# A feed-forward layer's first products taken by blocks: seven 2x2x2 block products (Strassen's scheme) in place of eight

## The chip, the cores and the metric

One core of a Trainium2 chip runs the whole program. The metric is the device time of one execution in microseconds. TensorE (PE) multiplies, VectorE (DVE), ScalarE (ACT) and GpSimd (POOL) do the element-wise work, SyncE (SP) issues the DMAs. Weights and activations lie in SBUF, matmul results in eight PSUM banks of 128 x 512 fp32.

## The reference

Two layers over 512 latent tokens and 256 context tokens, width 1024. Each layer has a mixing part and a gated feed-forward part; the last layer computes the latent tokens alone. What the change touches is the feed-forward part of the last layer:

```python
def swiglu(h, w1, w3, w2):
    return (jax.nn.silu(h @ w1) * (h @ w3)) @ w2

x = x + g_f * swiglu(ada_modulate(x, norm_ffn, sh_f, sc_f), ffn_w1, ffn_w3, ffn_w2)
```

`h` is 512 x 1024, `w1` and `w3` are 1024 x 2816 (22 blocks of 128 features), `w2` is 2816 x 1024. `ada_modulate` is an RMS norm with a scale and a shift per channel.

## The kernel before

Activations lie feature-major: a tile holds 128 channels by all tokens, and there are eight such tiles (k = 0 to 7). Every fp32 product is made of three TensorE matmuls in the fp32r format: each operand is split into a high part (an ACT copy, rounded) and a low part (source less high part, a DVE or POOL subtraction), and `mm3` (line 181) adds high x high, low x high and high x low into one PSUM bank:

```python
def mm3(o, lh, ll, rh, rl, start, stop):
    mm(o, lh, rh, start, False)
    mm(o, ll, rh, False, False)
    mm(o, lh, rl, False, stop)
```

The helpers `mm` (L179 in the profile), `tt` (L187), `stt` (L190) and `act` (L193) stand for nearly all instructions, so the profile is read by tiles more than by lines. `split` (line 195) is the ACT copy and the subtraction.

The feed-forward part (from line 1281) runs in three parts of the 22 features, `FF_PARTS` (line 32): first the w1 and w3 products of the part's features, with a gate after each (`gate_up`, line 1326: tanh on ACT, two DVE multiplications, a split into a `g` tile), then the part's w2 products, whose sums are added to the residual tiles `xl` on DVE. A w1 or w3 product of one feature block is 8 k-steps of `mm3` over 512 tokens: 24 matmuls of 512 columns into one bank (`up_k`, line 1321). Weights come by `fload` and `w13` (lines 1293 and 1296): a DMA on SP's queue into a `raw` tile of 128 x 1024 (a ring of 3), then a split into a `whl` tile (a ring of 6 in the last layer). The w2 weights come in the same way.

The start of the last layer's feed-forward part is by halves of 256 tokens, since its input is made by halves: the mixing part's output projection ends with the products of the second half (from line 1262), while the norm of the first half is already summed up (`norm_add`, `norm_sums`, `norm_spread`, lines 361 to 395) and its tiles are modulated (`norm_mod`, line 405). Two feature blocks are multiplied with the first half, then the norm of the second half is spread by a matmul, then the same two with the second half. The first weights (`W_first`, line 1304) are loaded early, at the priority of the projection, and their low parts are made on POOL.

A planner (the tile framework, with a simulated time line) sets the order of instructions on each engine from the order of the program, priorities and its own estimates; the feed-forward part has no order of TensorE written out by hand. Each engine's queue, and SP's, then runs in that order. Rings (`bufs` of a pool) give a tile out again when all that used it is done.

## Time and profile before

| what | value |
|---|---|
| runs (3) | median 1691.22 us, 1690.29 to 1695.56 |
| the profiled execution | 1694.43 us |
| its span | 1692.6 us, 25083 instructions |
| granted TensorE clock, mean | 0.988 |
| TensorE matmuls | 1638.8 us busy, 97% of the span, 9924 recorded |
| DVE, ACT, POOL | 920.2, 578.6 and 238.7 us busy |
| last layer's feed-forward part | 1325.66 us to the end of the span, 366.94 us |

Busy time is the union of an engine's instructions, without its waits for semaphores. In a time line, consecutive instructions of one group are merged into a row: start, length, engine, line, operation, out<-in with shapes, count, and in brackets the idle time before it with what ended it. A table by stage gives, for each stretch, its length and then the busy time and count of each engine, the granted clock, the DMA share and the rate. A group row gives busy time and mean nanoseconds of one.

### The profile page before, as it was taken

Reading aid. Unit: us, or ns where it says so; the run is one execution under the profiler, and the core shown is the slowest. Engines: PE = TensorE matmul, PEld = TensorE weight load, DVE = VectorE, ACT = ScalarE, POOL = GpSimd, SP = SyncE. Lnnn points to the kernel's source line nnn. Section 1 sums busy time; section 2 is a strip of 40 time slices with the busy share of each in tenths; the row PEclk is TensorE's granted clock in tenths of the full one; section 3 lists DMA queues with packets and bytes.
Section 4 is the critical chain, followed back from the end, with each engine's and each line's share of the span. In section 5 each row is a group of like instructions: output and inputs, shape, how many; then the busy total and the mean of one; then the engine's idle time right before and its main releaser. Section 6 shows DMA issues by size and latency. Waiting matters only on the chain.

```text
span 1692.6 us, 25083 instructions
## 1 busy us (share of the span) xinstructions
PE 1638.8 (97%) x9924; PEld 1418.1 (84%) x9924; DVE 920.2 (54%) x1651; ACT 578.6 (34%) x1023; POOL 238.7 (14%) x280
## 2 busy tenths in 40 slices
PE   6999999799899999999999999999989899999999
PEld 5888988688788888888888889899777888888887
DVE  5799765677755563553433443453567553343332
ACT  4474224445434311221122324831445432222220
POOL 0143431003212300000000011332102200000000
PEclk9999999899899999999999999999999999999999
DMA  9545535834033362442411301322773143223321
GB/s 326 172 153 162 179 97 163 231 85 129 30 125 125 125 187 88 135 146 79 138 63 55 117 35 39 94 80 71 201 181 116 56 137 100 90 90 106 101 85 52
DMA packets 81394, 200.66 MB, mean 119 GB/s; under 512 B 10680, under 2 KB 26876, under 8 KB 80252
## 3 DMA queue, kind: packets, MB, share of 16 engines
q1 hardware_dynamic: 81276, 199.06, 38.0%
q8 instruction: 78, 1.28, 0.3%
q14 instruction: 40, 0.33, 0.1%
HBM read 172.81 MB, written 12.85 MB: 110 GB/s over the span
## 4 chain that ended last, share of the span: by engine, by line
PE 87%; DMA 4%; DVE 4%; ACT 2%; issue 1%; SPq 1%; POOL 0%; DVEq 0%; ACTq 0%; POOLq 0%
PE a L179 29%; PE m L179 25%; PE b L179 21%; PE y L179 11%; PE b L1184 1%; DMA st<-kt 1%; DVE u L190 1%; DVE whl L187 1%; DMA st<-qt 1%; DMA vn<-scr_v 0%; DVE adac L190 0%; DVE nacc L187 0%; DMA qn<-scr_q 0%; DMA adaw<-in_ada 0%; DMA raw<-in_wg 0%
## 5 line engine op out<-in xcount | busy, mean ns | idle before, releaser
L193 ACT ACTIVATE whl<-raw 128x1024 fp32r<-128x1024 f32 (+7 forms) x222 | 204.8, 927 | 386.9 <-PE a L179 142.6
L179 PE MATMUL m<-u,whl 128*128 128x512 f32 (+1 forms) x1278 | 266.5, 360 | 1.9 <-DVE whl L187 1.3
L187 DVE TENSOR_TENSOR whl<-raw,whl 128x1024 fp32r<-128x1024 f32 (+7 forms) x201 | 224.5, 1118 | 79.7 <-ACT whl L193 79.5
L179 PE MATMUL a<-u,whl 128*128 128x512 f32 (+1 forms) x1299 | 248.2, 347 | 3.1 <-ACT u L193 2.4
L179 PEld LDWEIGHTS m<-u,whl 128*128 128x128 f32 x1278 | 213.0, 192 | 36.4 <-DVE whl L187 1.9
L179 PEld LDWEIGHTS a<-u,whl 128*128 128x128 f32 x1299 | 210.0, 190 | 34.7 <-ACT u L193 2.8
L179 PE MATMUL b<-u,whl 128*128 128x512 f32 (+1 forms) x915 | 184.2, 352 | 3.1 <-DVE whl L187 1.8
L190 DVE SCALAR_TENSOR_TENSOR adac<-adaw,u,adac 128x512 f32<-128x512 f32 x196 | 158.0, 828 | 34.4 <-DMA adaw<-in_adaw 33.2
L179 PEld LDWEIGHTS b<-u,whl 128*128 128x128 f32 x915 | 151.6, 192 | 26.7 <-DVE whl L187 2.4
L179 PE MATMUL b<-whl,u 128*128 128x384 f32 (+1 forms) x696 | 144.4, 343 | 1.7 <-DVE u L190 0.9
L179 PE MATMUL m<-whl,u 128*128 128x384 f32 (+2 forms) x672 | 140.3, 344 | 0.5 <-ACT u L193 0.5
L179 PEld LDWEIGHTS b<-whl,u 128*128 128x128 f32 x696 | 122.0, 188 | 8.2 <-issue 3.9
L179 PE MATMUL a<-g,whl 128*128 128x512 f32 (+1 forms) x594 | 126.7, 370 | 0.0
L179 PEld LDWEIGHTS m<-whl,u 128*128 128x128 f32 x672 | 116.0, 188 | 12.1 <-issue 7.9
L179 PEld LDWEIGHTS a<-g,whl 128*128 128x128 f32 x594 | 103.9, 189 | 19.4 <-DVE ft L190 0.8
L190 DVE SCALAR_TENSOR_TENSOR ft<-ft,a 128x512 f32<-128x512 f32 (+1 forms) x53 | 30.5, 575 | 99.7 <-ACT ft L193 65.3
L179 PE MATMUL y<-u,whl 128*128 128x512 f32 (+1 forms) x420 | 82.5, 349 | 0.1
L179 PEld LDWEIGHTS y<-u,whl 128*128 128x128 f32 x420 | 68.1, 189 | 12.2 <-issue 1.7
L179 PE MATMUL m<-g,whl 128*128 128x512 f32 (+1 forms) x396 | 77.8, 350 | 0.0
L187 POOL TENSOR_TENSOR nacc<-nacc,nsq 128x256 f32<-128x256 f32 (+1 forms) x21 | 21.0, 1001 | 391.4 <-ACT nsq L193 391.2
L179 PEld LDWEIGHTS m<-g,whl 128*128 128x128 f32 x396 | 64.7, 189 | 9.7
L179 PE MATMUL b<-g,whl 128*128 128x256 f32 (+1 forms) x396 | 72.5, 336 | 0.0
(207 smaller groups left out, 2004.7 us busy)
## 6 DMA issues: line engine op xcount, KB each, us to landing
raw<-in_w SPq DMA_DIRECT2D x104, 512.0 KB, 3.7
adaw<-in_adaw SPq DMA_DIRECT2D x48, 512.0 KB, 4.7
adaw<-in_adaw SPq DMA_DIRECT2D x64, 256.0 KB, 2.8
raw<-in_wg SPq DMA_DIRECT2D x40, 384.0 KB, 3.6
raw<-in_w SPq DMA_DIRECT2D x32, 448.0 KB, 3.3
st<-kt SPq DMA_DIRECT2D x48, 192.0 KB, 6.2
adaw<-in_ada SPq DMA_DIRECT2D x8, 1024.0 KB, 10.0
raw<-in_woa SPq DMA_DIRECT2D x16, 320.0 KB, 5.4
```

The lines of the kernel that those rows point to most:

```text
L179: T.matmul(o, lhsT=l, rhs=r, start=start, stop=stop, skip_group_check=True)
L187: e.tensor_tensor(out=o, in0=a, in1=b, op=op)
L190: V.scalar_tensor_tensor(out=o, in0=a, scalar=s, in1=b, op0=op0, op1=op1)
L193: S.activation(out=o, in_=i, func=f, **kw)
L1184: T.transpose(ps[:, 128 * j:128 * j + 128], p[:, 128 * j:128 * j + 128], ident)
```

## The change

In the last layer, a new function `feed_forward_blocks` takes the place of the whole feed-forward part. It takes the features by pairs (11 pairs). For each pair, the matrix (2 feature blocks) x (2 halves of the 1024 channels) is multiplied with the matrix (2 halves of the channels) x (2 halves of the tokens) by Strassen's scheme in Winograd's form: seven products of blocks instead of eight, with sums of weight blocks (S) and of activation blocks (T) made before, and sums of products made after. A block product is, for w1 and w3 (w) and four k-steps (i), one `mm3` over 256 columns, 24 matmuls; both w lie in one bank.

- Weights: a pair loads four chunks of 128 x 1024 (`chunk`); POOL makes s3 = a11 - a21, s1 = a21 + a22, then S2 = s1 - a11 and S4 = a12 - S2 in place; each of the seven is split by ACT and DVE (`unit`). The `raw` ring has 6 places, the ring of split units (`wu`) 4.
- Activations: the T operands of the seven products are made once (`ops`), from `scaled`, `shifted` and `plain`, and kept.
- Sums of products: three banks X, Y, Z per pair. X takes products 1, 6, 7 and 4 in turn, Z products 5 and 3; between them ACT takes snapshots (`snap`), and DVE and POOL add a bank or a snapshot to another into the tiles `cm`, on which the gate works.
- The first two pairs run together, product by product in the order 1, 2, 5, 6, 3, 7, 4, so that the first two products need the first half of the tokens only; their first weights lie in spare `g` tiles and are split on POOL. The other pairs run one by one in the order 1, 5, 6, 2, 7, 3, 4.
- The parts are 8, 8 and 6 features instead of 8, 7 and 7, in both layers.

The diff, cut where a step is plain:

```diff
-FF_PARTS = ((0, 8), (8, 15), (15, 22))
+FF_PARTS = ((0, 8), (8, 16), (16, 22))
...
+        def feed_forward_blocks():
...
+            gtile = lambda: mk(gpool, [128, 2, TL], F32R, "g", 8)
+            def chunk(f, kh, spare=False):
+                raw = flat(gtile()).bitcast(F32) if spare else mk(wp, [128, 1024], F32, "raw", 6)
+                nc.sync.dma_start(out=raw, in_=d["w13"][l, f, :, :, 4 * kh:4 * kh + 4])
+                return raw
+            def unit(raw, e=V):
+                u = mk(wp, [128, 2, 1024], F32R, "wu", 4)
+                n = raw.shape[-1]
+                split(raw, u[:, 0, :n], u[:, 1, :n], e)
+                return u[:, :, :n].rearrange("p q (w k c) -> p q w k c", w=2, c=128)
+            class Pair:
+                def __init__(self, p, kinds, spare=False, e=V):
+                    self.p, self.kinds = p, kinds
+                    self.a11, self.a12 = chunk(2 * p, 0, spare), chunk(2 * p, 1, spare)
+                    self.u = {}
+                    if spare:
+                        self.u[1], self.u[2] = unit(self.a11, e), unit(self.a12, e)
+                    self.cm = [mk(tp, [128, 2, 2, 256], F32, "cm", 2) for _ in range(2)]
+                def rest(self):
+                    a21, a22 = chunk(2 * self.p + 1, 0), chunk(2 * self.p + 1, 1)
+                    if 1 not in self.u:
+                        self.u[1] = unit(self.a11)
+                    s3 = mk(wp, [128, 1024], F32, "raw", 6)
+                    tt(G, s3, self.a11, a21, ALU.subtract)
+                    tt(G, a21, a21, a22, ALU.add)
+                    self.s1, self.s3, self.a22 = a21, s3, a22
+                def weights(self, n):
+                    if n == 6:
+                        tt(G, self.a11, self.s1, self.a11, ALU.subtract)
+                    if n == 3:
+                        tt(G, self.a12, self.a12, self.a11, ALU.subtract)
+                    if n not in self.u:
+                        self.u[n] = unit({2: self.a12, 3: self.a12, 4: self.a22, 5: self.s1, 6: self.a11, 7: self.s3}[n])
+                    return self.u.pop(n)
...
+                def after(self, n):
+                    ab = lambda a: a.rearrange("p (w c) -> p w c", w=2)
+                    if n == 1:
+                        self.snap("p1", self.X)
+                    if n == 5:
+                        self.snap("p5", self.Z)
+                    if n == 6:
+                        self.snap("u1", self.X)
+                    if n == 2:
+                        tt(V, self.cm[0][:, :, 0], ab(self.Y), ab(self.p1), ALU.add)
+                    if n == 7:
+                        self.snap("u2", self.X)
+                        tt(G, self.cm[1][:, :, 1], ab(self.u2), ab(self.p5), ALU.add)
+                    if n == 3:
+                        tt(V, self.cm[0][:, :, 1], ab(self.Z), ab(self.u1), ALU.add)
+                        self.gate(0)
+                    if n == 4:
+                        act(self.cm[1][:, :, 0], ab(self.X), AF.Copy)
+                        self.gate(1)
...
+            def products(pairs, n, outer=False):
+                us = [p.weights(n) for p in pairs]
+                bs = [p.bank(n) for p in pairs]
+                for iis in [(i,) for i in range(4)] if outer else [range(4)]:
+                    for p, u, (bank, first) in zip(pairs, us, bs):
+                        for w in range(2):
+                            for i in iis:
+                                mm3(bank[:, 256 * w:256 * w + 256], u[:, 0, w, i], u[:, 1, w, i], ops[n][i][:, 0],
+                                    ops[n][i][:, 1], first and w == i == 0, i == 3)
+                for p in pairs:
+                    p.after(n)
...
+            products(two, 1, True)
+            sums = norm_sums((accs[1], 256), np0)
+            for p in two:
+                p.rest()
+            products(two, 2, True)
+            rb2 = norm_spread(sums, np0)
+            for i in four:
+                scaled(i, 1, 0, rb2)
+                tt(V, t[i][:, 0], t[i][:, 2], t[i][:, 0], ALU.subtract)
+                plain(5, i, 0)
+            products(two, 5, True)
+            for i in four:
+                scaled(i, 1, 1, rb2)
+                shifted(3, i, 3)
+                stt(t[i][:, 2], t[i][:, 3], between[:, i:i + 1], t[i][:, 2], ALU.add, ALU.subtract)
+                stt(t[i][:, 3], t[i][:, 3], sh(i + 4), t[i][:, 0], ALU.add, ALU.subtract)
+                plain(6, i, 3)
+            products(two, 6, True)
+            products(two, 3)
...
+            for pi, (f0, f1) in enumerate(FF_PARTS):
+                for p in range(f0 // 2, f1 // 2):
...
+                    q = Pair(p, {"X": bank, "Y": bank, "Z": bank})
+                    q.rest()
+                    for n in (1, 5, 6, 2, 7, 3, 4):
+                        products([q], n)
...
```

What is left out: the gate, which works as before but from the `cm` tiles; `shifted` (ACT adds the shift, DVE makes the low part) and `plain` (a split); the T operands of products 7 and 4; and the w2 stage, which loads its weights by halves of the part's features instead of by output blocks and is the same otherwise.

## Rows read from the trace of the kernel before

**Rows 1.** Page: TensorE's busy time, and the chain that ended last by engine.

```profile
PE 1638.8 (97%) x9924; PEld 1418.1 (84%) x9924; DVE 920.2 (54%) x1651; ACT 578.6 (34%) x1023; POOL 238.7 (14%) x280
...
PE 87%; DMA 4%; DVE 4%; ACT 2%; issue 1%; SPq 1%; POOL 0%; DVEq 0%; ACTq 0%; POOLq 0%
```

**Rows 2.** Table by stage: start, w1/w3 of part two, last w2, sum.

```profile
1325.66:1373.06 47.40, 46.28 (x297) 42.15 (x298) 28.14 (x57) 18.84 (x34) 1.86 (x3) 1.00 0.26 83
...
1460.10:1536.26 76.16, 76.16 (x338) 63.07 (x337) 29.79 (x34) 20.82 (x27) 0.00 (x0) 1.00 0.29 90
...
1650.49:1692.60 42.11, 38.25 (x169) 31.34 (x167) 10.54 (x13) 3.38 (x4) 0.00 (x0) 1.00 0.13 51
sum 366.94, PE 361.96 PEld 303.23 DVE 148.20 ACT 94.06 POOL 1.86; mean PE 51.71 PEld 43.32 DVE 21.17 ACT 13.44 POOL 0.27
```

**Rows 3.** Time line of TensorE: 68 matmuls of 256 columns, then groups of 512.

```profile
1345.60 8.32 PE L179 MATMUL a<-u,whl 128*128 128x256 f32 x68
1353.76 4.27 PE L179 MATMUL b<-u,whl 128*128 128x512 f32 x18
...
1460.10 5.60 PE L179 MATMUL b<-u,whl 128*128 128x512 f32 x24
1465.54 5.60 PE L179 MATMUL m<-u,whl 128*128 128x512 f32 x24
```

**Rows 4.** Time line of TensorE, start: first matmul, second norm's spread, first operand.

```profile
1325.66 0.50 PE L179 MATMUL b<-u,whl 128*128 128x256 f32 x2 [0.91 <-ACT u L193]
...
1337.91 0.61 PE L179 MATMUL a<-ndg,u 128*128 128x128 f32 x4
...
1339.62 0.74 PE L179 MATMUL a<-u,whl 128*128 128x256 f32 x4 [1.11 <-ACT u L193]
```

**Rows 5.** Time lines of POOL (two rows), then of DVE over the same time.

```profile
1304.49 2.40 POOL L187 TENSOR_TENSOR whl<-raw,whl 128x1024 fp32r<-128x1024 f32 x1 [8.50 <-ACT whl L193]
1307.23 4.96 POOL L187 TENSOR_TENSOR whl<-raw,whl 128x1024 fp32r<-128x1024 f32 x2 [0.34 <-ACT whl L193]
...
1307.49 0.47 DVE L190 SCALAR_TENSOR_TENSOR u<-b,u,u 128x256 f32<-128x256 f32 x1
1307.88 2.04 DVE L187 TENSOR_TENSOR nacc<-nacc,nsq 128x256 f32<-128x256 f32 x1
...
1310.25 2.22 DVE L187 TENSOR_TENSOR nacc<-nacc,nsq 128x256 f32<-128x256 f32 x1
...
1312.79 0.41 DVE L187 TENSOR_TENSOR nacc<-nacc,nsq 128x256 f32<-128x256 f32 x1
```

**Rows 6.** Groups by form: DVE, ACT; last, POOL's 128x512 (minimum/median/maximum ns).

```profile
L187 DVE TENSOR_TENSOR whl<-raw,whl 128x1024 fp32r<-128x1024 f32 x46 | 56.3, 1225 | 23.6 <-ACT whl L193 23.6
L187 DVE TENSOR_TENSOR g<-ft,g 128x512 fp32r<-128x512 f32 x20 | 13.7, 683 | 0.0
L190 DVE SCALAR_TENSOR_TENSOR ft<-ft,a 128x512 f32<-128x512 f32 x15 | 10.3, 688 | 44.6 <-ACT ft L193 31.1 <-PE a L179 13.4
L190 DVE SCALAR_TENSOR_TENSOR nt<-u,u,rb 128x512 f32<-128x512 f32 x8 | 6.0, 752 | 0.4
L190 DVE SCALAR_TENSOR_TENSOR u<-nt,u,u 128x256 fp32r<-128x256 f32 x16 | 7.3, 488 | 0.8 <-ACT u L193 0.8
L193 ACT ACTIVATE whl<-raw 128x1024 fp32r<-128x1024 f32 x104 | 109.6, 1056 | 248.7 <-PE a L179 97.3 <-PE m L179 63.3 <-PE b L179 32.7
L193 ACT ACTIVATE ft<-a 128x512 f32<-128x512 f32 x17 | 10.2, 597 | 58.2 <-PE a L179 58.2
L187 POOL TENSOR_TENSOR asum<-u,u x10: 1284/1290/1747, 175.1 to 1179.7; 128x512 f32<-128x512 f32 x10
```

**Rows 7.** DMA issues: KB each, median us from issue to landing.

```profile
raw<-in_w SPq DMA_DIRECT2D x104, 512.0 KB, 3.7
```

**Rows 8.** Time line of TensorE at the border of the layers.

```profile
1007.31 0.79 PE L179 MATMUL b<-whl,u 128*128 128x384 f32 x3 [0.89 <-DVE u L190]
```

More of the change, by code (lines that the diff above doesn't have):

```diff
@@ L1281, in hybrid_kernel @@
+        if last:
+            feed_forward_blocks()
+            xst.close()
+            continue
         p4_ = ExitStack()
```

71 lines of the change are left out of this document (added).

## Prediction

> **What bounds the kernel now.** I read the page first. TensorE is busy for 97% of the span and holds 87% of the chain that ended last [rows 1]. Then the table by stage, cut where the last layer's feed-forward begins and at its parts: the granted clock is 1.00 (the 2.4 GHz level) in each stage, and TensorE is busy for 46.28 of the first 47.40 us, all of a w1/w3 stage and all but the output tail of the last stage [rows 2]. So in this stretch of 366.94 us only fewer or shorter matmuls help, unless something new makes TensorE wait. The TensorE timeline gives the pace: a group of 24 matmuls of 512 columns starts 5.44 us after the one before, 226.7 ns each; the 68 matmuls of 256 columns that begin at 1345.60 end with the next group at 1353.76, 120.0 ns each [rows 3]. Last I read VectorE (DVE) and GpSimd (POOL) where both work, since the change gives both much to do.
>
> **What TensorE saves.** The change touches the last layer's 11 pairs of features. A pair took 2x2x8x3 = 96 matmuls of 512 columns, 21.76 us; seven block products of 2x4x3 = 24 matmuls of 256 columns are 168, 20.16 us (2.88 us a product). Ten pairs save 1.60 us each; the first, which already ran as 192 matmuls of 256 columns (23.04 us), saves 2.88. Together 18.9 us. The w2 products are as many as before (8x22x3), so their three stages and the tail stay at 123.7 us.
>
> By the Trainium skill (TensorE: Matmul & The Clock Gate, "Back-to-back issue gap") an isolated matmul's spacing is columns / 2.4 + 2.5 ns, 215.8 and 109.2 ns; by that the saving would be 26.3 us. The rows have about 13 ns above the columns' own time, which weighs on twice as many instructions; they decide, and the sum stays at 18.9.
>
> **What is added, and where it lies.** A steady pair (the nine after the first two) now gives POOL four additions of 128x1024 and one of 128x512; DVE seven weight splits (four before), two additions of a PSUM bank to a snapshot, four multiplications and two splits for the gates; ScalarE (ACT) seven weight copies and five copies out of PSUM besides the gates. Alone, no engine is full in 20.16 us: DVE 7x1.225 + 2x0.688 + 4x0.752 + 2x0.683 = 14.3 us, ACT about 7x1.056 + 9x0.6 = 12.8, POOL 4x2.40 + 1.28 = 10.9 [rows 5, 6].
>
> But DVE and POOL don't run freely side by side. A DVE addition of 128x256 with both inputs in SBUF takes 0.41 us alone; the two that met a POOL addition of 128x1024 took 2.04 and 2.22 us, and the second ended 0.28 us after POOL's second (1312.47 against 1307.23 + 4.96 = 1312.19). A DVE operation of the same width that reads PSUM, begun at 1307.49 in the middle of it, took its usual 0.47 [rows 5]. So a POOL addition and a DVE operation with two SBUF inputs exclude each other. Of DVE's work above all but the two PSUM additions is of that kind. The share of the time that really excludes: DVE's duration less 0.13 us (0.41 less 0.28), POOL's (4.96 less 0.28) / 2 = 2.34. A pair then needs 7x1.10 + 4x0.62 + 2x0.55 + 4x2.34 + 1.28 = 21.9 us of the shared way into SBUF, against 20.16 us of TensorE; with the full durations it is 12.95 + 10.9 = 23.8. The w2 stages soften that: during one, TensorE has 38 to 44 us of work and the two engines little, so the first pair of parts two and three finds its four POOL results and two splits ready (11.6 us). Four pairs of a part then need 4x21.9 - 11.6 - 1.8 (the last gate, after the last product) = 74.2 us of 80.6. By the sum the shared way just suffices; what is left is the order in time.
>
> **The chain through a steady pair.** The raw ring has 6 places and a pair uses 5, the split ring 4 for 7 units. So the sixth unit of a pair (for product 3) waits until product 5, the second, is done; its split frees the raw place into which the next pair's second chunk column is loaded; SP's queue is in order, so the load behind it waits too. Chain from the end of product 5 to the next pair's product 5: copy 1.06 and split 1.22, load 3.7, two POOL additions 4.8, copy 1.06, split 1.22: 13.1 us [rows 5 to 7]. The room is six products, 17.3 us. Contention adds to it: each of the two POOL additions may wait for a DVE operation (up to 1.1 each), the last split waits for the third POOL addition (begun while ACT copies; +1.3) and, if the gate's two dependent multiplications of the pair before stand ahead of it in DVE's order, for the fourth as well (+3.0), and the hops between engines cost about 1. That is 15.4 at best and 20.6 at worst, so TensorE stalls 0 to 3.3 us a pair. I take 1.4, just under the middle, for the seven pairs with no w2 stage before them: 9.8 us (0 to 23).
>
> **The first two pairs.** Here the T operands are made too. Before, four features took 47.40 us [rows 2], 44.8 by the pace and 2.6 of stalls (the second half of the tokens: its norm is spread at 1337.91 and TensorE waits 1.11 us for the first operand [rows 4]). After, by the pace, 14 products are 40.3 us. Time below runs from the first matmul at 1325.66. Products 1 and 2 use the first 256 tokens and ended at 12.25 before (the spread); eight POOL additions (what the pairs' `rest`, product 6 and product 3 need) may now get in the way of the eight DVE operations that make their low halves. With none in the way 12.25 stands; with all, 8x2.34 + 8x0.488 + 1.44 = 24. POOL can do most of them before or while TensorE has work queued, so I take 14.5. Then DVE is the limit: two PSUM additions 1.4, the operands of product 5 4x(0.47 + 0.41 + 0.41) = 5.2, those of products 6 and 3 4x(0.47 + 3x0.49 + 0.41) = 9.4, four splits of which one is done ahead 3.7, less some overlap: 19.2 us [rows 5, 6], where TensorE has 11.5 of work (products 5 and 6). With 0.6 us for the spread and 1.4 for the last twelve matmuls, product 6 ends at 35.7; products 3, 7 and 4 take 17.3: 53.0, which is 5.6 later than before. The ends: 47.5 (+0) if product 2 ends at 12.25 and product 3 fills TensorE's waits, and 62.5 (+15).
>
> **Small terms.** A gate ends about 0.7 us later behind its last product (one more ACT copy); the first w2 chain needs that feature last and can switch to the next bank, so 0 to 0.7 for each of three parts. The parts 8, 8, 6 hold for the first layer too: there the last w2 products of the latent tokens, which cover the context tokens' norm for the next layer, shrink by 4x3x226.7 ns = 2.7 us, at a border where TensorE already waits 0.89 us [rows 8]. Together 1.4 (0 to 4.8). Chunks now come as runs of 2 KB instead of 4 KB; their number and bytes are the same, and SP issues nothing else here.
>
> **Sum.** Pairs three to eleven save 9x1.60 = 14.4. Change: +5.6 - 14.4 + 9.8 + 1.4 = +2.4 us. The profiled run took 1694.43 us (span 1692.6 and 1.8 around it), so it would be 1696.9; against the median of the runs, 1691.22, it is 1693.6. The savings of TensorE would be given back, nearly whole, to waits on DVE and POOL.
>
> **The rivals.** *Hidden after all (faster).* The list order places POOL's additions early and DVE's splits ahead of the gates, so that the chain closes within its 17.3 us and product 3 fills the start. For it: 13.1 us without contention, and w2 stages that pay for 11.6 us. Then the start costs 1, a pair 0.5: 1 - 14.4 + 3.5 + 1 = -8.9, 1682 (1675 to 1687).
>
> *The shared way is the bound (slower).* Every pair without a w2 stage before it takes 23.8 us, as operations wait for the whole of the other engine's instruction. It decides once the sum of both engines' SBUF work passes 21.76, what a pair cost before; the two bounds, 21.9 and 23.8, are on that side. Against it: the work ahead in the w2 stages. Seven pairs at 3.64 us are 25.5, the start +10: 10 - 14.4 + 25.5 + 1.4 = +22.5, 1714 (1700 to 1722).
>
> The Trainium skill (SBUF — State Buffer, "SBUF: two separate sides") calls the port pair of DVE and GpSimd an exclusive lock, held for the whole instruction, also against a DVE operation with two SBUF inputs. The 2.04 and 2.22 us rows agree; that the holder's last 0.13 us still overlap is the measured part.
>
> *The saving is not there.* If 256 columns cost more than 21.76 / 168 = 129.5 ns in products that change bank and weights every 24 matmuls, nothing is saved. 68 in a row at 120.0, whose weights change with each one, speak against it. At 132 ns it is +22, 1716.
>
> **How the numbers follow.** Forecast 0.46 (1687 to 1700), hidden 0.29, shared way 0.21, no saving 0.04. A measurement tells about 0.3% (5.1 us) from no change, 1686.1 to 1696.3. Of the forecast's span some seven tenths lie inside, 0.33, and 0.13 above; hidden gives 0.28 faster and 0.01 inside; the last two are slower. Faster 0.28, same 0.34, slower 0.38. The range leaves a third of the hidden case below 1680 and the upper part of the slow ones above 1711.
>
> **What would show it.** In the trace after: 256-column groups 2.88 us apart inside a product (the saving); POOL additions of 128x1024 above 2.40 and splits above 1.225 us (the exclusion); idle time of TensorE ended by DVE's split, once a pair at product 5 or 6 (the chain), and some 13 us of it between product 2 and the end of product 6 of the first pairs; a period of 20.2 us in the first pair after a w2 stage and of about 21.5 in the others. Wrong it would be if TensorE stays above 98% busy from the third pair on, or if the periods pass 23 us.

## The result and the profile after

| | before | after |
| --- | --- | --- |
| median of four runs each, one chip (us) | 1690.76 | 1713.24 (1708.86 to 1717.85) |
| ratio, 95% interval | | 1.0108 (1.0083 to 1.0133) |
| profiled execution: span (us), granted clock | 1692.6, 0.988 | 1709.2, 0.980 |

The kernel is slower, by 1.1% by the ratio and by 1.3% (22.5 us) by the two medians. The forecast was 1693.6 (1680 to 1711). The median lies 2.2 us above that range; the ratio, taken on the 1691.22 us that the forecast started from, gives 1709.5, which is 1.5 us inside it. Either way the change is +18 to +22 us where +2.4 was forecast. On the page of after, TensorE is busy for 9.5 us less than in [rows 1], but that is 95% and not 97% of the span, and holds 83% of the chain instead of 87%.

```profile
PE 1629.3 (95%) x10620; PEld 1443.1 (84%) x10620; DVE 1043.4 (61%) x1731; ACT 645.2 (38%) x1121; POOL 378.2 (22%) x335
...
PE 83%; DVE 6%; DMA 4%; issue 2%; ACT 2%; SPq 1%; POOL 0%; DVEq 0%; ACTq 0%; POOLq 0%
```

Where the time went is seen in a table by stage that starts where the attention's last value product ends, before the feed-forward (columns: stretch and its length, busy time and count of PE, PEld, DVE, ACT, POOL, granted clock, DMA share, GB/s). The rows are: to the first feed-forward matmul; part one; part two; part three with its w2 stage and the last update (the last 3.1 us of each span are left out). First before, which the prediction cut only at the first feed-forward matmul:

```profile
1301.96:1325.66 23.70, 20.51 (x141) 19.90 (x140) 17.54 (x32) 13.00 (x25) 15.90 (x11) 0.86 0.35 117
1325.66:1460.09 134.43, 133.31 (x680) 114.22 (x681) 62.19 (x94) 40.35 (x59) 1.86 (x3) 1.00 0.29 93
...
sum 387.56, PE 382.47 PEld 323.13 DVE 165.73 ACT 107.06 POOL 17.77; mean PE 95.62 PEld 80.78 DVE 41.43 ACT 26.77 POOL 4.44
```

Then after:

```profile
1300.45:1331.01 30.56, 21.99 (x141) 21.25 (x141) 21.44 (x32) 9.79 (x19) 22.13 (x12) 0.79 0.36 121
1331.01:1481.87 150.86, 131.39 (x873) 121.95 (x873) 115.43 (x136) 68.67 (x104) 54.48 (x24) 0.93 0.24 77
1481.87:1609.97 128.10, 125.17 (x865) 116.89 (x864) 90.66 (x76) 55.97 (x72) 50.44 (x20) 1.00 0.31 99
1609.97:1706.07 96.10, 93.81 (x649) 87.42 (x647) 61.52 (x59) 39.04 (x53) 28.98 (x12) 1.00 0.27 86
sum 405.62, PE 372.37 PEld 347.51 DVE 289.05 ACT 173.47 POOL 156.04; mean PE 93.09 PEld 86.88 DVE 72.26 ACT 43.37 POOL 39.01
```

The stretch is 18.1 us longer (405.62 - 387.56). The first row takes 6.9 more, part one 16.4 more; parts two and three, 229.43 before (387.56 less the two rows shown), take 5.2 less. So the scheme pays in parts two and three, and more than four times that gain is lost before them. The waits of TensorE, grouped by what it waited for (total, times, longest), in the whole stretch of after:

```profile
PE a L179 <- DVE ndg L401: 10.2, 4, 6.7
PE a L179 <- DVE nacc L187: 6.6, 1, 6.6
PE b L179 <- DVE wu L187: 5.1, 3, 2.2
PE m L179 <- ACT u L193: 4.3, 1, 4.3
PE m L179 <- DVE u L187: 2.7, 1, 2.7
```

`nacc` and `ndg` are the two norms (sum of squares, spread), `u` the operands of product 5, `wu` the weights' splits. The first two and the last two are the start. Before, the wait for the first norm (`nacc`) was 2.28 us, and the spread (`ndg`) was not waited for. The two rows of TensorE, before's first, then four of DVE's additions for this norm in after:

```profile
1315.23 1.01 PE L179 MATMUL a<-u,nacc 128*128 128x1 f32 x4 [2.28 <-DVE nacc L187]
...
1317.98 1.01 PE L179 MATMUL a<-u,nacc 128*128 128x1 f32 x4 [6.60 <-DVE nacc L187]
...
1306.32 2.48 DVE L187 TENSOR_TENSOR nacc<-nacc,nsq 128x256 f32<-128x256 f32 x1
1309.12 2.22 DVE L187 TENSOR_TENSOR nacc<-nacc,nsq 128x256 f32<-128x256 f32 x1
1313.11 2.33 DVE L187 TENSOR_TENSOR nacc<-nacc,nsq 128x256 f32<-128x256 f32 x1
1315.76 2.17 DVE L187 TENSOR_TENSOR nacc<-nacc,nsq 128x256 f32<-128x256 f32 x1
```

The next table cuts after's part one: up to the end of product 2, to product 5's first matmul, to the end of product 6, and to the end of the first two pairs:

```profile
1331.01:1344.60 13.59, 12.52 (x101) 12.25 (x100) 9.61 (x16) 8.28 (x16) 7.71 (x6) 0.98 0.01 1
1344.60:1358.90 14.30, 1.72 (x6) 1.00 (x4) 14.30 (x18) 5.07 (x8) 9.04 (x4) 0.64 0.23 73
1358.90:1375.25 16.35, 13.64 (x97) 13.35 (x97) 15.55 (x38) 9.22 (x21) 0.00 (x0) 0.79 0.00 0
1375.25:1394.90 19.65, 17.43 (x139) 17.23 (x138) 17.99 (x14) 10.35 (x15) 10.49 (x5) 0.95 0.25 82
```

Between products 2 and 5 DVE works without a pause for 14.30 us, and TensorE stands for 12.6 of them. In the third row its 96 matmuls would take 11.5 us at the pace of [rows 3]; 2.7 are a wait, and the 2.1 left over lie where the granted clock is at the lower level (1.2 GHz) at first, after TensorE stood. A row of two matmuls of 256 columns takes 0.63 us there and 0.40 a little later:

```profile
1364.71 0.63 PE L179 MATMUL m<-u,wu 128*128 128x256 f32 x2
...
1366.61 0.40 PE L179 MATMUL m<-u,wu 128*128 128x256 f32 x2
```

### The profile page after: what moved, and what is told of

It reads as the page before. It is cut to its first block, busy times and chain, and to the rows that moved or that the text cites. A ratio compares the mean times of both kernels' runs of the same rounds, so it can differ in the third digit from the quotient of the medians.

```text
span 1709.2 us, 26769 instructions
## 1 busy us (share of the span) xinstructions
PE 1629.3 (95%) x10620; PEld 1443.1 (84%) x10620; DVE 1043.4 (61%) x1731; ACT 645.2 (38%) x1121; POOL 378.2 (22%) x335
## 4 chain that ended last, share of the span: by engine, by line
PE 83%; DVE 6%; DMA 4%; issue 2%; ACT 2%; SPq 1%; POOL 0%; DVEq 0%; ACTq 0%; POOLq 0%
PE a L179 27%; PE m L179 24%; PE b L179 20%; PE y L179 10%; DVE wu L187 2%; PE b L1184 1%; DMA raw<-in_woa 1%; DVE u L190 1%; DVE nacc L187 1%; DVE whl L187 1%; DMA u<-in_xt 1%; ACT whl L193 1%; DVE ft L190 0%; DVE adac L190 0%; DMA qn<-scr_q 0%
## 5 line engine op out<-in xcount | busy, mean ns | idle before, releaser
L193 ACT ACTIVATE whl<-raw 128x1024 fp32r<-128x1024 f32 (+6 forms) x154 | 134.8, 882 | 242.5 <-PE m L179 89.2
L187 DVE TENSOR_TENSOR wu<-raw,wu 128x1024 fp32r<-128x1024 f32 (+1 forms) x93 | 145.7, 1573 | 59.5 <-ACT wu L193 59.1
L187 DVE TENSOR_TENSOR whl<-raw,whl 128x1024 fp32r<-128x1024 f32 (+6 forms) x137 | 147.4, 1079 | 54.1 <-ACT whl L193 53.6
L190 DVE SCALAR_TENSOR_TENSOR adac<-adaw,u,adac 128x512 f32<-128x512 f32 x196 | 158.9, 832 | 34.5 <-DMA adaw<-in_adaw 33.3
L179 PE MATMUL a<-u,whl 128*128 128x512 f32 (+1 forms) x843 | 153.0, 337 | 2.1 <-ACT u L193 1.3
L179 PEld LDWEIGHTS a<-u,whl 128*128 128x128 f32 x843 | 130.7, 192 | 19.1 <-ACT u L193 1.5
L187 POOL TENSOR_TENSOR raw<-raw,raw 128x1024 f32<-128x1024 f32 x38 | 105.5, 2777 | 172.6 <-DVE wu L187 71.5
L193 ACT ACTIVATE wu<-raw 128x1024 fp32r<-128x1024 f32 (+1 forms) x93 | 95.5, 1036 | 104.3 <-POOL raw L187 33.1
L179 PEld LDWEIGHTS m<-whl,u 128*128 128x128 f32 x672 | 115.9, 188 | 12.6 <-issue 8.0
L187 POOL TENSOR_TENSOR nacc<-nacc,nsq 128x256 f32<-128x256 f32 (+1 forms) x21 | 21.2, 1010 | 397.8 <-ACT nsq L193 397.5
L179 PE MATMUL b<-u,wu 128*128 128x256 f32 x552 | 76.0, 288 | 6.1 <-DVE wu L187 5.1
L179 PE MATMUL m<-u,wu 128*128 128x256 f32 x528 | 72.9, 287 | 7.0 <-ACT u L193 4.3
L179 PE MATMUL a<-u,wu 128*128 128x256 f32 x576 | 75.6, 285 | 0.9 <-DVE wu L187 0.9
```

The source lines that it names most:

```text
L179: T.matmul(o, lhsT=l, rhs=r, start=start, stop=stop, skip_group_check=True)
L187: e.tensor_tensor(out=o, in0=a, in1=b, op=op)
L190: V.scalar_tensor_tensor(out=o, in0=a, scalar=s, in1=b, op0=op0, op1=op1)
L193: S.activation(out=o, in_=i, func=f, **kw)
```

## What DVE did while TensorE stood

The time line of DVE in after, from the end of product 1 on, and under it that of POOL over the same time (start, duration, idle time before it and what ended that):

```profile
1339.91 1.23 DVE L187 TENSOR_TENSOR wu<-g,wu 128x1024 fp32r<-128x1024 f32 x1 [3.80 <-ACT wu L193]
1341.31 0.16 DVE L389 TENSOR_SCALAR nms<-a 128x2 f32<-128x2 f32 x1 [0.18 <-PE a L179]
1341.39 3.31 DVE L187 TENSOR_TENSOR wu<-g,wu 128x1024 fp32r<-128x1024 f32 x1
1344.63 1.21 DVE L187 TENSOR_TENSOR wu<-raw,wu 128x1024 fp32r<-128x1024 f32 x1
...
1346.37 2.77 DVE L187 TENSOR_TENSOR wu<-raw,wu 128x1024 fp32r<-128x1024 f32 x1
...
1349.66 4.06 DVE L401 TENSOR_SCALAR ndg<-u,nrs 128x128 f32<-128x128 f32 x2
1353.64 1.21 DVE L187 TENSOR_TENSOR wu<-g,wu 128x1024 fp32r<-128x1024 f32 x1
1354.78 3.21 DVE L190 SCALAR_TENSOR_TENSOR g<-u,u,a 128x256 f32<-128x256 f32 x8
...
1341.22 2.41 POOL L187 TENSOR_TENSOR g<-raw,g 128x1024 f32<-128x1024 f32 x1 [2.05 <-DVE wu L187]
1343.59 1.69 POOL L187 TENSOR_TENSOR nrs<-nms,u 128x2 f32<-128x2 f32 x1
1345.26 2.80 POOL L187 TENSOR_TENSOR g<-raw,g 128x1024 f32<-128x1024 f32 x1
1348.02 5.62 POOL L187 TENSOR_TENSOR g<-g,g 128x1024 f32<-128x1024 f32 x2
```

Three things meet. The splits at 1341.39 and 1346.37 end 1.1 us after a POOL sum has ended, and the spread at 1349.66 ends 0.1 us after one, as if they had been held until then (3.31 and 2.77 for 1.22; 4.06 for 0.47). The queue holds work for later products ahead of the first operand of product 5: a split for product 6 at 1353.64, and among the eight scaled tiles at 1354.78 the four of product 6. And the splits at 1339.91 and 1341.39 have no reader: `rest` runs after product 1 has taken the pair's first unit, finds it gone, and splits it a second time.

## The experiments

Theories, under letters that not all texts on record use: the exclusion of POOL sums and DVE operations costs the time (E); the order in DVE's queue does (O); there is more DVE work at the start than TensorE work to cover it, wherever the sums stand (W). The times to the end of part one (the first two rows of the table by stage) and of parts two and three, from each run's own trace; medians beside the kernel before on the same chip:

| run | to the end of part one, against 158.13 before | parts two and three, 229.43 before | median (before) |
| --- | --- | --- | --- |
| after | 181.42 (+23.3) | 224.20 | 1713.24 (1690.76) |
| parts 8, 8, 6 alone | 157.64 (-0.5) | 229.42 | 1694.37 (1695.9), one run |
| no sums on POOL | 165.30 (+7.2) | 218.30 | 1693.81 (1695.9) |
| all sums on DVE | 172.98 (+14.9) | 218.29 | 1698.1 (1695.9) |
| sums of the first two pairs on DVE | 175.49 (+17.4) | 225.05 | 1711.07 (1695.9) |
| after without the double splits | 181.04 (+22.9) | 225.33 | 1710.46 (1695.21) |
| all on DVE without the double splits | 171.79 (+13.7) | 218.29 | 1697.5 (1695.21) |
| all on DVE, order written out | 191.44 (+33.3) | 218.29 | 1716.94 (1695.21) |
| first pair plain | 166.02 (+7.9) | 218.29 | 1689.31 (1695.21) |
| first pair plain, start in order | 160.71 (+2.6) | 218.30 | 1687.2 (1694.2) |
| the same, steady sums on POOL | 166.05 (+7.9) | 223.90 | 1695.86 (1694.2) |
| first two pairs plain | 153.03 (-5.1) | 218.30 | 1678.8 (1692.98) |

**The parts alone.**

```diff
-FF_PARTS = ((0, 8), (8, 15), (15, 22))
+FF_PARTS = ((0, 8), (8, 16), (16, 22))
```

> The kernel before with the feed-forward parts 8, 8, 6 alone. In the changed kernel the work around the end of the last layer's attention stood 1.5 us earlier in the trace than before (1301.95 against 1303.46). Theory A, it comes from the parts: the same group of matmuls begins 1 to 2 us earlier here, and the span is about 1691. Theory B, it comes from a new plan of the order or from the run: it begins within 0.5 us of before, span about 1692.6.

The first feed-forward matmul came at 1325.57 us (1325.66 before), the span was 1692.6 in both. The parts cost nothing, and the shift of 1.5 us that the attention's end shows between the traces of before and after is not theirs. Whether it comes from a new plan or from the execution isn't shown; over all the traces that end lies between 1297.6 and 1307.7.

**No sums on POOL.** The weight sums are left out (the splits take unsummed weights), s3 and one sum of products are constants.

```diff
-                    tt(G, s3, self.a11, a21, ALU.subtract)
-                    tt(G, a21, a21, a22, ALU.add)
+                    G.memset(s3, 0.5)
...
-                        tt(G, self.a11, self.s1, self.a11, ALU.subtract)
...
-                        tt(G, self.a12, self.a12, self.a11, ALU.subtract)
...
-                        tt(G, self.cm[1][:, :, 1], ab(self.u2), ab(self.p5), ALU.add)
+                        G.memset(self.cm[1][:, :, 1], 0.5)
```

> The changed kernel without the sums on GpSimd: weight blocks go into the products unsummed, s3 and one sum of products are filled with a constant; all matmuls, splits and T operands stay. Theory A, exclusion: the additions on GpSimd hold back the norm's sums, its diagonals and the splits on VectorE at the start; without them the start is 15 to 22 us shorter and the time is 1690 to 1698 us. Theory B, VectorE's own work and the order in its queue make the start late: the start is shorter by under 6 us, the time above 1705.

The ratio was 0.9979 (0.9961 to 0.9998): 2.1 us under the kernel before where after is 22.5 above it. The time and the start (181.42 to 165.30, 16.1 us) lie where theory A had them. Rows by stage of this run: parts two and three have TensorE busy all the time but for the last update.

```profile
1305.26:1331.18 25.92, 19.98 (x142) 19.21 (x141) 17.89 (x30) 10.68 (x22) 14.92 (x11) 0.87 0.42 143
1331.18:1470.56 139.38, 128.28 (x872) 119.86 (x873) 91.49 (x138) 68.15 (x102) 9.00 (x10) 0.96 0.26 84
1470.56:1594.75 124.19, 124.19 (x866) 116.67 (x864) 69.57 (x76) 55.90 (x72) 5.74 (x8) 1.00 0.32 102
1594.75:1688.86 94.11, 93.32 (x649) 87.31 (x647) 50.46 (x59) 39.31 (x53) 3.37 (x5) 1.00 0.28 87
```

The sums cost all that the forecast gave them and more. But part one still is 5.0 us longer than before, where TensorE saves 2.88 + 3x1.60 = 7.7: with no sum at all it loses 12.6 us. In this run POOL still makes the four first splits, and DVE the two splits without a reader, so the 12.6 are not DVE's needed work alone.

**All sums and the first splits on DVE.**

```diff
-                    tt(G, s3, self.a11, a21, ALU.subtract)
+                    tt(V, s3, self.a11, a21, ALU.subtract)
```

and so for the other four, and for the engine of the first four splits.

> All of GpSimd's sums and first splits in the new part go to VectorE. Theory A, exclusion: a 128x1024 sum takes 1.2 us there and holds nobody up; the start gets 10 to 18 us shorter, a steady pair has 19.9 us of VectorE work in 20.2 us of TensorE and may lose 0 to 2 us; time 1693 to 1705. Theory B, VectorE's own work: it gets 12 additions or splits of 1.2 us more at the start and is full in the pairs, the time grows by 8 us or more, to 1721 and above.

The ratio was 1.0017 (0.9996 to 1.0037). The time lies in theory A's range; the start got 8.4 us shorter, not 10 to 18. The groups by form show the exclusion gone: a split took 1630 ns on the mean in after and 1221 here (rows: after's DVE and POOL, then this run's splits and sums, both DVE):

```profile
L187 DVE TENSOR_TENSOR wu<-raw,wu 128x1024 fp32r<-128x1024 f32 x85 | 138.2, 1630 | 53.1 <-ACT wu L193 52.7
L187 POOL TENSOR_TENSOR raw<-raw,raw 128x1024 f32<-128x1024 f32 x38 | 105.5, 2777 | 172.6 <-DVE wu L187 71.5 <-issue 48.2 <-DVE cm L187 28.3
```

```profile
L187 DVE TENSOR_TENSOR wu<-raw,wu 128x1024 fp32r<-128x1024 f32 x85 | 103.4, 1221 | 44.2 <-ACT wu L193 44.0
L187 DVE TENSOR_TENSOR raw<-raw,raw 128x1024 f32<-128x1024 f32 x38 | 46.5, 1222 | 6.5 <-DMA raw<-in_w 2.8 <-issue 2.4 <-DVE g L187 0.9
```

A sum takes 1.22 us of DVE; made by POOL it held a split up by as much as 2.1 (3.31 for 1.22). In parts two and three nothing waits any more. At the start TensorE still waits, 7.6 us for the first norm and 10.6 between products 2 and 5, where it was 6.6 and 12.6 in after.

**Sums of the first two pairs on DVE**, the others and the first splits on POOL.

```diff
+                    self.p, self.kinds, self.e = p, kinds, V if spare else G
...
-                    tt(G, s3, self.a11, a21, ALU.subtract)
+                    tt(self.e, s3, self.a11, a21, ALU.subtract)
```

> Only the sums of the first two pairs go from GpSimd to VectorE; their first splits and the other pairs stay on GpSimd. Theory A, exclusion: the start gets 10 to 18 us shorter and the steady pairs stay as they are, 1695 to 1703. Theory B, VectorE's own work: eight additions of 1.2 us more in its queue, 1720 or more.

The start gave 5.9 us in the trace (181.42 to 175.49) and the medians some 7 (1711.07 against 1695.9, 15.2 above, where after is 22.5 above), less than the 10 to 18 that E wanted; the ratio was 1.0078 (1.0055 to 1.0101). TensorE waits the same 7.6 and 10.6 us as in the run before, where no sum stood on POOL. So E alone does not account for the start. Against the run with all sums on DVE, the steady pairs' sums on POOL, with the first four splits, cost 400.54 - 391.27 = 9.3 us in the stretch.

**The double splits**, taken out of after and out of the run on DVE.

```diff
-                    if 1 not in self.u:
+                    if self.p > 1:
                         self.u[1] = unit(self.a11)
```

> The changed kernel, with one thing less: rest() no longer splits the first unit of the first two pairs a second time. Product 1 has taken those units by then, so that rest() makes two splits that nothing reads: on VectorE (DVE) at 1339.91 (1.23 us) and 1341.39 (3.31 us, beside a GpSimd sum of 2.41), with two copies of 1.06 us on ScalarE, ahead of the spread of the second norm. Theory D (the double splits are a good part of the lost start): DVE is free 4.5 us earlier, the idle time of TensorE between products 2 and 5 (12.6 us) falls to some 8, and the total by 4 to 5 us, to about 1709 where the changed kernel stands at 1713. Theory X (exclusion alone): the GpSimd sums only move into the free time and block what stands there, the idle time stays within 1.5 us, and the total within 2 us of 1713.

> The run with all sums and first splits on VectorE (1698.1 us), without the double splits and with nothing else changed. Theory D: two splits of 1.22 us fewer ahead of the spread and the operands of product 5, so the idle time of 10.6 us ahead of product 5 falls by about 2.4 and the total to about 1695.7. Theory O: the time falls by less than 1, since other sums and splits move up into the same place.

In after the idle time between products 2 and 5 fell from 12.6 to 9.2 us, near to what D wanted, but the first row grew by 1.7, the stretch changed by less than 1 us (406.37 and 405.62), and the ratios overlap (1.0092, 1.0069 to 1.0115). On DVE the wait ahead of product 5 fell from 10.6 to 5.4 us, but other sums moved up ahead of the first norm, whose wait rose from 7.6 to 10.8; the medians differ by 0.6. The double splits stood in the way; taking them out alone gained nothing that the runs can tell from noise.

**The order of DVE's queue written out**, all sums on DVE, no double splits.

```diff
+            with tc.manual_schedule(engines={mybir.EngineType.DVE}):
+                for p in two:
+                    p.load_rest()
+                for n, r in ((1, 0), (2, 1)):
+                    ahead(lambda i: scaled(i, 0, r, rb), lambda i: shifted(n, i, r))
+                products(two, 1, True)
+                for p in two:
+                    p.rest()
...
+                    p.u[5] = unit(p.s1)
+                rb2 = norm_spread(sums, np0)
+                products(two, 2, True)
+                ahead(lambda i: scaled(i, 1, 0, rb2), t1)
+                products(two, 5, True)
...
```

> All sums on VectorE (DVE) as before in the run with 1698.1 us, no double splits, the first four splits on GpSimd again, and from the first operand to product 4 of the first two pairs DVE follows the order of the text: operands of products 1 and 2, the two sums of each pair, their splits for product 5, the spread, then the four operands of product 5 and of product 6 in turn, sums and splits for products 6 and 3 behind them. Theory O (what is left at the start is the order in DVE's queue): the wait ahead of the first norm falls from 7.6 to about 2.5 us, that between products 2 and 5 from 10.6 to under 3, nothing comes in their place, and the total is about 1686. Theory W (the start simply holds too much DVE work): from the first operand to product 4 DVE has about 50 us of work (8 sums and 10 splits of 1.2, some 20 us of operands, the rest gates) where TensorE has 40.3, so what is saved ahead of product 5 comes back ahead of products 6, 3 and 7; only the 5 us of the first norm and the 2.4 of the double splits stay, and the total is 1691 to 1695.

The ratio was 1.0133 (1.0106 to 1.016), no better than after; the stretch is 4.1 us longer (409.73). The wait ahead of product 5 did fall, to 1.87 and 2.25 us at the spread and the operand, but this stands in its place on the time line of TensorE:

```profile
1363.95 0.58 PE L179 MATMUL m<-u,wu 128*128 128x256 f32 x1 [13.33 <-ACT wu L193]
...
1388.15 5.28 PE L179 MATMUL m<-u,wu 128*128 128x256 f32 x23 [8.91 <-DVE wu L187]
1404.62 4.33 PE L179 MATMUL m<-u,wu 128*128 128x256 f32 x23 [5.02 <-DVE wu L187]
```

The time came back ahead of product 6 and of later ones, as W says, and more than it, since a strict order also waits out each hop to ACT and back (DVE's splits show idle times of 1.1 us ended by ACT's copy). So the total is 22 us or more above what W gave as well. The wait of 13.33 us ends with ACT's copy for product 6's first split, and this order puts the sum that the copy reads behind all operands of products 5 and 6. The run speaks against O, but it shows one order that was bad, not that none is good.

**The first pair plain.** Features 0 and 1 by eight plain block products in halves of the tokens, as before; their T operands are not needed, and the second pair's are made meanwhile. All sums on DVE.

```diff
-                two = [Pair(0, {"X": PM, "Y": PB, "Z": PM}, True, G), Pair(1, {"X": PB, "Y": PY, "Z": PA}, True, G)]
+                first = [[unit(chunk(f, kh, True), G) for kh in range(2)] for f in range(2)]
...
+            bs = plain_half(0, (1, 2))
...
+            half_gates(0, bs)
+            bs = plain_half(1, (7, 3))
```

> All sums on VectorE (DVE); the first pair of features is taken by eight plain block products, two halves of the tokens one after the other as in the kernel before (192 matmuls of 256 columns, 23.04 us, no sums, no T operands), and the second pair is the first by seven; its operands are made while TensorE works on the first. It gives up 2.88 us of TensorE. Theory W: DVE now has 43 us of TensorE work (23.0 and 20.2) over its 40 or so and needs the T operands only 20 us later; the start costs what it did in the kernel before (about 1.1 us of idle time in the first part), and ten pairs save 1.6 us each: 1676 to 1682 where the kernel before is at 1691 to 1696. Theory O: no better than the run with the order written out, or worse by the 2.88, some 1686 to 1690, as the queue is left to the planner here too.

The ratio was 0.9966 (0.9951 to 0.9981): faster than before, less than W expected, and in the range that O gave (1686 to 1690), though O took it from a written order at some 1686, which came to 1716.94. 7.1 us of waits were left in part one, and the granted clock was at the lower level from 1346.0 to 1356.3.

**Its start in another order.** Feature by feature, the fourth split and the second pair's sums after the operands of the first half, T operands after those of the second.

```diff
+                first = [[unit(chunks[f][kh], G) for kh in range(2 - f)] for f in range(2)]
...
+                first[1].append(unit(chunks[1][1]))
...
+                plain_half(0, b0[0], (1, 2))
+                sums = norm_sums((accs[1], 256), np0)
+                plain_half(1, b0[1], (1, 2))
```

> The run with the plain first pair (1689.3 us), with its start put in another order: the first half feature by feature with the second norm's sums between the two, the fourth unit's split and the first two sums of the second pair on VectorE (DVE) only after the eight operands of the first half, and the operands of the second half ahead of the T operands, in the written order on DVE. Theory Q (what is left of the loss at the start is the order in DVE's queue, with the half clock that follows): there TensorE waited 5.0 us ahead of the first norm and 9.1 - 2.0 = 7.1 in the first part, and ran at half clock from 1346 to 1356; the kernel before had 2.3 and 1.1 there. The wait for the norm falls to about 2.5, those of the first part to about 2, and with the half clock some 8 us go: 1681 to 1683. Theory W (the start has too much DVE work in any order): the waits move behind the first pair, ahead of products 1 to 6 of the second, and the time stays within 2 us of 1689.

The ratio was 0.9963 (0.9946 to 0.9981). The stretch fell by 5.3 us (384.31 to 379.01), as Q says in part, but in the medians the two runs can't be told apart (1689.31 and 1687.2, within the 2 us of W). Of the waits left, 1.4 us stand in the first pair, ahead of the second half's first operand, and 5.4 in the second pair, as W says:

```profile
1344.32 0.51 PE L179 MATMUL m<-u,wu 128*128 128x256 f32 x2 [1.42 <-ACT u L193]
1365.54 3.13 PE L179 MATMUL a<-u,wu 128*128 128x256 f32 x24 [0.45 <-ACT snap L193]
1369.86 0.39 PE L179 MATMUL a<-u,wu 128*128 128x256 f32 x1 [1.19 <-ACT wu L193]
1373.98 4.39 PE L179 MATMUL a<-u,wu 128*128 128x256 f32 x23 [3.73 <-DVE wu L187]
```

**The steady sums back on POOL**, in that kernel.

```diff
-                    tt(V, s3, self.a11, a21, ALU.subtract)
+                    tt(V if self.p < 2 else G, s3, self.a11, a21, ALU.subtract)
```

and so for the other four sums.

> The same kernel with the sums of the pairs three to eleven on GpSimd again, as in the changed kernel; its start is untouched. It prices the sums on GpSimd in the steady pairs alone. The comparison of parts two and three between the changed kernel (128.1 and 95.2 us) and the one with all sums on VectorE (124.2 and 93.2) gives 5.9 us for seven pairs; with the two steady pairs of part one it should be 6 to 8 us more than the kernel beside it, with waits of 0.9 to 1.6 us ended by VectorE's split once a pair. My forecast put it at 9.8. If GpSimd helped by taking work from VectorE, it would be faster instead.

Medians 8.7 us apart (1695.86 and 1687.2), stretches 10.9 (389.95 and 379.01), a little above what was expected. Parts two and three give 5.6 us for five pairs (223.90 - 218.30), 1.1 each. In part one the wait of 3.73 us in the second pair grew to 6.87 as well, so 3.1 of the 10.9 us belong to the start and not to the steady pairs.

**The first two pairs plain.** Features 2 and 3 by 256-column blocks as well, so that the seven T operands are needed only after 46 us of TensorE work.

```diff
+            for f in (2, 3):
+                raws = [chunk(f, kh) for kh in range(2)]
+                us, bs = [unit(r) for r in raws], [bank() for _ in range(2)]
+                for kh in range(2):
+                    for h in range(2):
+                        for i in four:
+                            for w in range(2):
+                                o = ops[((1, 2), (7, 3))[h][kh]][i]
...
```

> The run with the plain first pair and the written order, with the second pair taken by eight plain block products of 256 columns as well (23.04 instead of 20.16 us of TensorE), so that the T operands are first needed after 46 us of TensorE work instead of 26. In the run before it TensorE waited 5.4 us in the second pair (0.5, 1.2 and 3.7 ahead of weights) and 1.4 ahead of the second half's first operand; DVE had no pause from 1350 to 1382. Theory W (too much DVE work per TensorE time at the start): the 5.4 us go, only the 1.4 stays, the first part gets 5.4 - 2.9 = 2.5 us shorter, to about 136.1, and the total is 2 to 3 us less. Theory Q (order alone): a wait of 3 us or more for a weight's split stays, the first part is at 139 or above, and the total is 2 to 3 us more. The times lie too near each other for the medians alone; the waits decide.

The ratio was 0.9922 (0.9901 to 0.9943): 1678.8 us, 0.8% under the kernel before. By stage, and the waits of TensorE in the whole stretch:

```profile
1297.61:1317.79 20.18, 17.47 (x141) 16.93 (x140) 15.18 (x30) 11.25 (x23) 12.33 (x10) 1.00 0.68 236
1317.79:1450.64 132.85, 131.55 (x920) 123.58 (x921) 98.26 (x156) 58.43 (x95) 1.80 (x3) 1.00 0.25 80
```

```profile
PE a L179 <- DVE nacc L187: 2.7, 1, 2.7
PE m L179 <- ACT u L193: 1.1, 1, 1.1
PE m L179 <- DVE u L190: 0.2, 1, 0.2
```

It gives up 2.88 us of TensorE against the run with one plain pair in order, and is 7.7 us shorter by the end of part one all the same (160.71 to 153.03); the waits in the second pair are gone, and the granted clock is 1.00 from the attention's end on. This is what W said, and more of it: part one takes 132.85 us, where W gave about 136.1. Not all of the gain over the kernel before is due to the seven products. In the trace 3.5 us lie ahead of the first feed-forward matmul (20.18 against 23.70), and there the wait for the norm is not shorter (2.66 us against 2.28); only the granted clock behind it did not fall. Behind waits of 2.28, 2.31 and 2.66 us the first row's clock was 0.86 in before, 0.93 with the parts alone and 1.00 here, so this part looks like the chance of an execution. The kernel before was not tried with this start. The profiled execution is also the fastest of its six (1673.82 us). What the pairs give in this trace is 11.1 us in parts two and three and 1.6 in part one.

## Why the prediction was right or wrong

The forecast of nearly no change was wrong, and the step that failed is the start, the first two pairs and what stands ahead of them. That the time lies so near the upper end of the range is luck: the range reached that far for the two slower rivals, and neither is what happened. By its steps, in the sums of the stretch (the forecast's from its own terms):

| | before | forecast | after |
| --- | --- | --- | --- |
| attention's end to the first feed-forward matmul | 23.70 | 23.70 | 30.56 |
| first four features | 47.40 | 53.0 | 63.89 |
| rest of part one | 87.03 | 86.6 | 86.97 |
| parts two and three, small terms | 229.43 | 226.6 | 224.20 |
| sum | 387.56 | 389.9 | 405.62 |

- **TensorE's saving: right.** Groups of 24 matmuls lie 2.88 us apart, and with nothing in the way parts two and three take 218.30 instead of 229.43: 11.1 us for seven pairs, 1.59 each (1.60 forecast).
- **The exclusion: right in kind.** Splits take 1.63 us and sums 2.78 on the mean in after, 1.22 and 2.40 alone.
- **The steady pairs: right in size.** 9.8 us were forecast for seven pairs. After itself gives about 9.0: 5.9 in parts two and three (224.20 - 218.30) and 3.1 in the rest of part one (86.97, against 87.03 less two savings of 1.60). The two traces that differ in these sums alone give 10.9 (with 3.1 in the second pair) and 8.7 in their medians. The waits for a split come four times in after, 0.89 to 1.59 us each, not once in each of the seven pairs, and none in the first pair after a w2 stage. The sign set against the forecast, TensorE above 98% busy from the third pair on, came out on the edge (305.06 of 311.17 us, 98.0%).
- **The small terms: too high.** The parts cost nothing, and with nothing in the way parts two and three lose nothing to the gates (218.30, where 229.43 less seven savings of 1.60 is 218.23); 1.4 was put down for both.
- **The start: wrong, and the step that failed.** It was forecast at +5.6 us with an end of +15; it is +16.5, and +6.9 stand ahead of the first feed-forward matmul, where the sum had no term at all. First, "time below runs from the first matmul": I looked for collisions only behind it, though `early_w` and `rest` let POOL run its splits and the pairs' sums from 1302.9 to 1327.7, beside the first norm's additions on DVE, four of which took 2.48, 2.22, 2.33 and 2.17 us (two did in before [rows 5]). The wait for that norm was 2.28 us before and 6.60 after, and its spread was waited for as well (1.96 us). Second, the 19.2 us of DVE work between products 2 and 6 were put together from what these products need, as if DVE did nothing else first. From product 2's end to product 6's it was to be 21.2 us; it was 30.65, and DVE was busy for 29.85 of them. The spread was put down with the 0.6 us of its matmuls, and took DVE 4.06 us; there were six splits (8.9 us) where I had three (3.7), as two for product 3 stood in the queue, the one meant to be done ahead was not, and one waited 1.55 us for a POOL sum. Ahead of product 2's end DVE had made the two splits without a reader instead, which `rest` shows in the diff and I read past. Third, I gave a wait no price beyond its length; where the clock was lower behind it, 2.1 us more went.
- **The rivals.** 1714 was the rival in which the shared way is the bound, and the time agrees with it, but not the way: its pairs at 3.64 us were 1.2 to 1.6, its start at +10 was +23. For the start W fits best, as the last of the waits went only when the sums and T operands were taken out of it. E has a part: with no sum anywhere part one lost 12.6 us, with the sums and first splits on DVE 7.7 more go by its end (165.30 to 172.98), with them on POOL another 8.4 (181.42).

Still open: how the 8.4 us divide between the exclusion and the planner's order, which changes with every edit (the double splits show it). O is not ruled out: an order that gets the first two pairs by seven products through the start was not found, but only one was tried, and the plain first pair gained 5.3 us in the trace by its order alone.

## What to carry to other kernels

A scheme that trades matmuls for element-wise work is priced in two places: where it is steady, by each engine's work in a period, and at its start, by how much of that work must be done before TensorE has anything else to do. Keep the plain products at the start until the extra operands can be made behind them, and keep the additions on the engine that already has the splits, if the two engines exclude each other. Read in the diff what is queued ahead of the step that is waited for, before its first instruction too.

## What the hardware showed that was not expected

The exclusion reaches further than the additions of [rows 5]. Two DVE operations of 128x128 that multiply one SBUF tile by a column (`ndg`) took 0.47 us alone, in before, and 4.06 beside two POOL sums in after:

```profile
1330.79 0.47 DVE L401 TENSOR_SCALAR ndg<-u,nrs 128x128 f32<-128x128 f32 x2
```

The forecast had counted only operations with two SBUF tiles. By the Trainium skill (VectorE: DVE Perf Modes, "Mode 2×_2P — use both read ports for one tensor") an fp32 operation of that kind can take both read ports, and by the Trainium skill (SBUF — State Buffer, "SBUF: two separate sides") a two-port operation locks against POOL like one with two inputs. The 4.06 us agree with that; no run here shows the ports themselves. A POOL operation waits as well: `nrs`, 128x2, took 0.73 us at 1319.27 and 1.69 at 1343.59, while the split that DVE had begun at 1341.39 ran on to 1344.70. DVE's operations that read PSUM kept their times in these stretches (0.68 at 1345.77 and 1349.06).
